# A hybrid transformer block: sums of squares from the feature-major x, the decay chain placed within the first projection

## The chip, the core and the metric

The kernel runs on one core of one Trainium2 chip, as one program. The time is device microseconds of one execution; the median of several is given. TensorE multiplies matrices, VectorE (DVE in the profile), ScalarE (ACT) and GpSimd (POOL) work element by element, and SyncE (SP) issues the loads.

## The reference

One block of a model works on 256 tokens of 2048 features, all in fp32. A token mixer joins a spatially gated MLP and a gated linear attention; cross attention to a memory and a convolutional feed-forward layer follow. What the change touches is at the start:

```python
h = rmsnorm(x, pre_norm_mix[l])            # x * rsqrt(mean(x*x) + 1e-6) * g
z = h @ w_in                               # all projections of the mixer
...
u, vs = jnp.split(gelu(z_sg), 2, axis=-1)
y_a = spatial_gating(u, layernorm(vs, sg_ln_g, sg_ln_b), sg_w, sg_b)
gate_logit = (g_lr @ gla_w_gate2 + gla_b_gate).astype(jnp.float32)   # rank 16
log_a = jnp.maximum(jax.nn.log_sigmoid(gate_logit) / GLA_TAU, GLA_LOG_DECAY_MIN)
...
bcum = jnp.cumsum(to_chunks(log_a), axis=3)    # chunks of 64 tokens
q_in = qc * jnp.exp(bcum); k_in = kc * jnp.exp(-bcum); k_st = kc * jnp.exp(b_last - bcum)
```

## The kernel before

The 256 tokens are two tiles of 128. The 2048 features are 16 groups (k) of 128 partitions, and x comes twice: as token rows (`x`) and feature-major (`xT`). Each fp32 product is made of three: weights and activations are split into a part `hi`, rounded by a cast on ScalarE (`split_half`, L89), and a rest `lo`, a subtraction on VectorE (L90). The products hi·hi, hi·lo and lo·hi are summed in PSUM (L106 to L108). The root mean square's factor is not applied to the activations: the products are made from x times the gain (`gain_x`, which fills `hT`), and the factor comes on afterwards, as a column per token tile (`rs`, tile `r_mix`) or, where tokens lie along the free axis, as a row copied to all partitions (`rbc`).

Weights come in units of 1 MB (three buffers). One unit is cut in two pieces of 1024 columns, so a piece is one cast, one subtraction and 12 matmuls of 512 columns. `hi` and `lo` have four buffers each: the cast of a piece reuses the buffer of the piece four before it.

The first stage is written out by hand (`tc.manual_schedule`): 8 rounds, each with one unit of `w_sgv`, for the half `v` of the gated MLP. In a round stand the load of a later unit, the splits, `square_x` and `load_x` of token rows of x, `later_loads` for constants, and 24 matmuls (L448). Behind the rounds come 16 matmuls for the gates' rank-16 input (`glr`, L452) and `row_bcast`, which makes `rbc` from the two columns by two fp32 matmuls with diagonals. Everything behind the stage is placed by a scheduler that orders each engine's instructions from the program and estimates of their times.

Next come the gelu of `v` with its layer norm (L467 to L483, on `vv`), and `tok_block(w_sg, 0)` and `(w_sg, 1)`, the half `u`, of eight pieces each. After each piece but the first, `tok_block` calls `step()`, which takes one function from the list `later`. There stand the four `gate` (two matmuls each, Abs on ScalarE and a minimum on VectorE), `decay` (Exp and Ln on 128x2048, subtraction, scale), `cums` (a scan along the tokens, then the differences that fill `E1`) and `powers(q)` (exponentials into `EK` and `E1`, one head a call). `powers` of heads 1 to 3 are called in the blocks of k and q, which follow.

Of the kernel before, what the change touches and what calls it, by code (L numbers as in the profile page):

```python
# [44 lines left out]
def block_kernel(ctx: ExitStack, tc: tile.TileContext, a, out):  # L45
# [269 lines left out]
    with ExitStack() as mix:  # L315
# [20 lines left out]
        with ExitStack() as st2:  # L336
            xp0 = pool(st2, "sp0", side="right")

            gmix = xp0.tile([P, KD], F32, name="gmix")
            xt = [xp0.tile([P, 2, S], F32, name=f"xt_{i}") for i in range(KD // 2)]  # L340
# [3 lines left out]
            gh1 = xp0.tile([48, S], F32R, name="gh1")  # L344
            g2 = uu[1][0:96, :]
            xh, ss4s, rs = {}, {}, []

            def load_xt(k, n, eng=nc.sync):
                eng.dma_start(out=xt[k // 2][:, k % 2:k % 2 + n, :], in_=a["xT"][:, k:k + n, :])

            def load_unit(parts=((slice(0, 2), slice(0, 2)),)):
                i = len(first)
# [1 line left out]
                for n, k in parts:  # L354
                    nc.sync.dma_start(out=first[i][:, n, k, :], in_=a["w_sgv"][i, :, n, k, :])

            def load_x(i):
                t, n = divmod(i, 4)
                xh[i] = xp0.tile([P, 512], F32, tag="xh", bufs=3, name=f"x0_{t}_{n}")
                nc.sync.dma_start(out=xh[i], in_=a["x"][t * P:(t + 1) * P, n * 512:(n + 1) * 512])  # L360

            def square_x(i):
                t, n = divmod(i, 4)
                if n == 0:
                    ss4s[t] = stat.tile([P, 4], F32, tag="ss4", name=f"ss4_mix_{t}")
                nc.scalar.activation(out=uu[0][:, 0:512], in_=xh[i], func=AF.Square, accum_out=ss4s[t][:, n:n + 1])
                if n == 3:
                    ss = stat.tile([P, 1], F32, tag="ss", name=f"ss_mix_{t}")
                    nc.vector.reduce_sum(out=ss, in_=ss4s[t], axis=AX.X)
                    rs.append(rstd_of(ss, 1.0 / D, f"mix_{t}", const.tile([P, 1], F32, name=f"r_mix_{t}")))  # L370

            def gain_x(k):
                split_psum(hT[:, k, 0, :], hT[:, k, 1, :], xt[k // 2][:, k % 2, :], scale=gmix[:, k:k + 1])

            def later_loads(i):
                if i == 3:
                    nc.sync.dma_start(out=ident, in_=a["eye"])
                    nc.sync.dma_start(out=cols, in_=a["cols"])
                if i == 5:
                    nc.sync.dma_start(out=sgw, in_=a["sg_wT"])  # L380
                    nc.gpsimd.affine_select(
                        out=sgw, in_=sgw, pattern=[[0, SGG], [1, P]], compare_op=ALU.is_ge,
                        fill=0.0, base=0, channel_multiplier=-1)
                if i == 4:
                    nc.sync.dma_start(out=wgr, in_=a["w_glr"])
                    nc.sync.dma_start(out=g2, in_=a["gate2"])
                if i == 6:
# [7 lines left out]
                    nc.sync.dma_start(out=lng, in_=a["sg_ln_g"].partition_broadcast(P))  # L395
                if i == 7:
                    nc.sync.dma_start(out=lnb, in_=a["sg_ln_b"].partition_broadcast(P))

            first = []
            with tc.manual_schedule():  # L400
                nc.scalar.dma_start(out=gmix, in_=a["cols"][:, C_MIX:C_MIX + KD])
                first.append(wpool.tile([P, 2, 2, 512], F32, tag="raw", bufs=3, name="raw"))
                for k in (0, 1):
                    for n in range(2):
                        nc.sync.dma_start(out=first[0][:, n, k, :], in_=a["w_sgv"][0, :, n, k, :])
                        if n == 0:
                            load_xt(k, 1)
                load_xt(2, 2, nc.scalar)
                load_unit([(slice(0, 2), k) for k in range(2)])
                load_xt(4, 2)  # L410
                load_unit()
                warm_up(10)
                pss = [[mm_psum(f"sg_{n}_{t}") for t in range(NT)] for n in (2, 3)]
                nx = 0
                for i in range(KD // 2):
                    if 1 <= i < KD // 2 - 2:
                        load_xt(2 * i + 4, 2)
                        load_unit()
                    hl = []
# [16 lines left out]
                    for j in sorted(xh):  # L436
                        if j >= nx:
                            square_x(j)
                    nx = len(xh)
                    for j in {2: (0, 1), 3: (2,), 4: (3, 4), 5: (5,), 6: (6, 7)}.get(i, ()):  # L440
                        load_x(j)
                    later_loads(i)
                    for k in (2 * i, 2 * i + 1):
                        c = slice(k % 2 * 512, (k % 2 + 1) * 512)
                        for n, (hi, lo) in enumerate(hl):
                            for j, (part, w) in enumerate(((0, hi), (1, hi), (0, lo))):
                                for t in range(NT):
                                    nc.tensor.matmul(pss[n][t], hT[:, k, part, t * P:(t + 1) * P], w[:, c],  # L448
                                                     start=k == 0 and j == 0, stop=k == KD - 1 and j == 2)
                ps = mm_psum("glr")  # L450
                for k in range(KD):
                    nc.tensor.matmul(ps[0:80, :], wg[:, k, :, :], hT[:, k, :, :], start=k == 0, stop=k == KD - 1)  # L452
                row_bcast(rs, rbc, "mix")
# [19 lines left out]

        for n, ps in enumerate(pss):
            sg_v(ps, n + 2)
        for t in range(NT):
# [8 lines left out]
        with ExitStack() as st2:  # L485
# [4 lines left out]
            nc.gpsimd.memset(keep, 1.0)  # L490
            nc.gpsimd.memset(keep[:, :, 0:1], 0.0)

            def gate(i):
                gps = aux_psum(f"gate_{i}")
                for j in range(2):
                    f = 2 * i + j
                    nc.tensor.matmul(gps[:, j * S:(j + 1) * S], gate2[:, f * P:(f + 1) * P], glr,
                                     start=True, stop=True)
                gv = gps.rearrange("p (f s) -> p f s", f=2)
                nc.scalar.activation(out=la[:, 2 * i:2 * i + 2, :], in_=gv, func=AF.Abs)  # L500
                nc.vector.tensor_scalar_min(mn[:, 2 * i:2 * i + 2, :], gv, 0.0)

            def decay():
                nc.scalar.activation(out=la, in_=la, func=AF.Exp, scale=-1.0)
                nc.scalar.activation(out=la, in_=la, func=AF.Ln, bias=1.0)
                nc.vector.tensor_tensor(out=la, in0=mn, in1=la, op=ALU.subtract)
                nc.vector.tensor_scalar(out=la, in0=la, scalar1=1.0 / 16.0, scalar2=-1.0, op0=ALU.mult, op1=ALU.max)

            def cums():
# [51 lines left out]
        with ExitStack() as st:  # L561
# [454 lines left out]
```

## Time and profile before

| what | value |
|---|---|
| time, median of 3 (lowest to highest) | 1661.28 us (1660.66 to 1661.56) |
| profiled execution: time, span | 1661.93 us, 1660.2 us |
| TensorE busy | 1646.9 us (99% of the span), 8086 matmuls |
| VectorE, ScalarE, GpSimd busy | 1042.1 us (63%), 846.1 us (51%), 39.8 us (2%) |
| HBM read | 314.08 MB, 190 GB/s over the span |

The profile's page gives busy times over the whole span. The ends of matmul records are modelled, so that the start of one matmul to the start of the next is the measure of TensorE's pace. A row of the timeline gives start, duration, engine, line, operation, out<-in, shape, a count where like rows are joined, and in brackets the engine's idle time before it and what ended it.

### The profile page before, as it was taken

What the parts mean: (1) busy time and instruction counts of PE and PEld (TensorE: products, weight loads), DVE (VectorE), ACT (ScalarE), POOL (GpSimd) and SP (SyncE); (2) the same over time, 40 slices, a digit from 0 to 9 for tenths busy, and PEclk for the clock granted to TensorE, in tenths of its full rate; (3) what the DMA queues carried; (4) which work ended last, traced back from release to release, by engine and by line L of the source; (5) the groups of instructions that cost most, each with busy time, mean ns of one, the idle gap of its engine ahead of it and who ended that gap; (6) DMA issues with size and microseconds to landing.
All of it is one profiled execution on the core that took longest, in us unless ns stands there. A gap on an engine that the chain in (4) does not pass through costs nothing.

```text
span 1660.2 us, 20835 instructions
## 1 busy us (share of the span) xinstructions
PE 1646.9 (99%) x8086; PEld 1374.8 (83%) x8086; DVE 1042.1 (63%) x1394; ACT 846.1 (51%) x1182; POOL 39.8 (2%) x128
## 2 busy tenths in 40 slices
PE   9999999999999999999999999999999999999998
PEld 7788888888888888888888888888888888888886
DVE  5777645555454545465766877877777787444444
ACT  6774444444444444455655756555555555344332
POOL 0100000000000000000002000000000000000000
PEclk9999999999999999999999999999999999999999
DMA  9545455445555554585542555555555555555553
GB/s 344 221 160 177 177 186 172 176 176 177 186 194 178 182 198 178 187 333 215 204 177 105 202 193 187 181 200 178 190 191 182 195 181 216 190 187 193 179 199 103
DMA packets 49139, 317.52 MB, mean 191 GB/s; under 512 B 5552, under 2 KB 6192, under 8 KB 12304
## 3 DMA queue, kind: packets, MB, share of 16 engines
q1 hardware_dynamic: 48752, 315.93, 53.4%
q8 instruction: 63, 1.03, 0.2%
q14 instruction: 36, 0.29, 0.1%
q10 hardware_dynamic: 288, 0.27, 0.0%
HBM read 314.08 MB, written 2.10 MB: 190 GB/s over the span
## 4 chain that ended last, share of the span: by engine, by line
PE 95%; DMA 2%; ACT 1%; issue 1%; DVE 1%; SPq 0%; DVEq 0%; POOLq 0%; POOL 0%; ACTq 0%
PE up L137 18%; PE up L138 10%; PE ffn L108 5%; PE ffn L107 5%; PE ffn L106 5%; PE m L108 4%; PE m L107 4%; PE m L106 4%; PE p L108 3%; PE p L106 3%; PE p L107 3%; PE mix L108 2%; PE mix L106 2%; PE og L107 2%; PE v L108 2%; PE og L106 2%
## 5 line engine op out<-in xcount | busy, mean ns | idle before, releaser
L90 DVE TENSOR_TENSOR lo<-raw,hi 128x1024 fp32r<-128x1024 f32 (+1 forms) x567 | 689.5, 1219 | 460.9 <-ACT hi L89 456.7
L89 ACT CAST hi<-raw 128x1024 fp32r<-128x1024 f32 (+1 forms) x568 | 590.5, 1043 | 534.4 <-PE ffn L107 133.6
L137 PE MATMUL up<-fT,hi 128*128 128x512 f32 x1320 | 467.3, 394 | 0.4 <-DVE fT L210 0.4
L138 PE MATMUL up<-fT,lo 128*128 128x256 f32 x1320 | 373.1, 283 | 0.0
L137 PEld LDWEIGHTS up<-fT,hi 128*128 128x128 f32 x1320 | 247.9, 188 | 54.3 <-DVE fT L210 0.7
L138 PEld LDWEIGHTS up<-fT,lo 128*128 128x128 f32 x1320 | 248.1, 188 | 3.9
L108 PE MATMUL ffn<-lo,act 128*128 128x512 f32 x352 | 140.1, 399 | 0.0
L107 PE MATMUL ffn<-hi,act 128*128 128x512 f32 x352 | 138.7, 394 | 0.0
L106 PE MATMUL ffn<-hi,act 128*128 128x512 f32 x352 | 138.0, 392 | 0.0
L893 ACT COPY hd<-up 128x256 f32<-128x256 f32 x88 | 32.7, 373 | 137.0 <-PE up L141 137.0
L106 PE MATMUL m<-hi,hT 128*128 128x512 f32 x256 | 101.4, 396 | 0.0
L108 PE MATMUL m<-lo,hT 128*128 128x512 f32 x256 | 101.3, 396 | 0.0
L107 PE MATMUL m<-hi,hT 128*128 128x512 f32 x256 | 101.1, 395 | 0.0
L894 DVE TENSOR_TENSOR hd<-up,hd 128x256 f32<-128x256 f32 x88 | 37.4, 425 | 72.4 <-ACT hd L893 72.4
L107 PEld LDWEIGHTS ffn<-hi,act 128*128 128x128 f32 x352 | 66.1, 188 | 17.2
L106 PEld LDWEIGHTS ffn<-hi,act 128*128 128x128 f32 x352 | 66.1, 188 | 15.7
L108 PEld LDWEIGHTS ffn<-lo,act 128*128 128x128 f32 x352 | 66.1, 188 | 15.3
L107 PEld LDWEIGHTS m<-hi,hT 128*128 128x128 f32 x256 | 48.1, 188 | 11.4
L108 PEld LDWEIGHTS m<-lo,hT 128*128 128x128 f32 x256 | 48.1, 188 | 11.4
L106 PEld LDWEIGHTS m<-hi,hT 128*128 128x128 f32 x256 | 48.1, 188 | 11.2
L897 ACT ACTIVATE cv<-hd,cols 128x256 f32<-128x256 f32 x88 | 52.7, 602 | 0.3
L106 PE MATMUL v<-hi,hT 128*128 128x512 f32 x128 | 51.1, 399 | 0.0
(301 smaller groups left out, 2480.1 us busy)
## 6 DMA issues: line engine op xcount, KB each, us to landing
raw<-in_w_up SPq DMA_DIRECT2D x88, 1024.0 KB, 4.8
raw<-in_w_dn SPq DMA_DIRECT2D x44, 1024.0 KB, 4.8
raw<-in_w_v SPq DMA_DIRECT2D x16, 1024.0 KB, 4.8
raw<-in_w_og SPq DMA_DIRECT2D x16, 1024.0 KB, 4.8
raw<-in_w_ma SPq DMA_DIRECT2D x16, 1024.0 KB, 4.8
raw<-in_w_mb SPq DMA_DIRECT2D x16, 1024.0 KB, 4.8
raw<-in_w_pb SPq DMA_DIRECT2D x16, 1024.0 KB, 4.8
raw<-in_w_o SPq DMA_DIRECT2D x16, 1024.0 KB, 4.9
```

Of the source, the lines that this page charges most:

```text
L89: nc.scalar.copy(out=hi, in_=raw)
L90: (eng or nc.vector).tensor_tensor(out=lo, in0=raw, in1=hi.bitcast(F32), op=ALU.subtract)
L106: nc.tensor.matmul(ps, xh, wh, start=first, stop=False)
L107: nc.tensor.matmul(ps, xl, wh, start=False, stop=False)
L108: nc.tensor.matmul(ps, xh, wl, start=False, stop=last)
L137: nc.tensor.matmul(*big, start=k == 0, stop=False)
L138: nc.tensor.matmul(*small, start=False, stop=False)
L893: nc.scalar.copy(out=hd[:, 2:], in_=ps[:, S:2 * S])
L894: nc.vector.tensor_tensor(out=hd[:, 2:], in0=ps[:, 0:S], in1=hd[:, 2:], op=ALU.add)
L897: nc.scalar.activation(out=cv, in_=hd[:, 2:], func=AF.Identity, scale=cols[:, w0 + 2:w0 + 3], bias=cols[:, C_CB + j:C_CB + j + 1])
```

## The change

It has three parts. The squares are summed from the feature-major `xT`, which is loaded anyway: one ScalarE Square for each pair of k (128x512), added up on VectorE into `acc`. Before the last k of the first projection `token_rstd` adds the two halves and multiplies by ones on TensorE, in fp32: twice 128x2 for the columns, once 128x256 for the row on all partitions. VectorE scales both, and GpSimd raises them to the power -0.5, 128x2 into `rr` and 128x256 into `rbc`. The loads of `x` in this stage, their Squares with accumulate and `row_bcast` go.

Second, loads of constants move behind other weight units, `xt` becomes one tile that is loaded in fewer pieces, and the selection on `sgw` stands behind the stage.

Third, the gates, `decay`, `cums` and all four `powers` are put in `later` ahead of block 0, the four gates as one function `gates`, and TensorE's order in block 0 is that of the program. The gates' sums stay in PSUM until `decay`, which takes the minimum in one operation with the subtraction. The layer norm comes into the program behind block 0.

```diff
+            acc = xp0.tile([P, 2, S], F32, name="acc")
+            msb = xp0.tile([P, S], F32, name="msb")
...
-            def load_x(i):
-                t, n = divmod(i, 4)
-                xh[i] = xp0.tile([P, 512], F32, tag="xh", bufs=3, name=f"x0_{t}_{n}")
-                nc.sync.dma_start(out=xh[i], in_=a["x"][t * P:(t + 1) * P, n * 512:(n + 1) * 512])
-
             def square_x(i):
...
+                sq = acc if i == 0 else xp0.tile([P, 2, S], F32, tag="sq", bufs=2, name="sq")
+                nc.scalar.activation(out=sq, in_=xt[:, 2 * i:2 * i + 2, :], func=AF.Square)
+                if i > 0:
+                    nc.vector.tensor_tensor(out=acc, in0=acc, in1=sq, op=ALU.add)
+
+            def token_rstd():
+                nc.vector.tensor_tensor(out=acc[:, 0, :], in0=acc[:, 0, :], in1=acc[:, 1, :], op=ALU.add)
+                tot = aux_psum("tot")
+                for t in range(NT):
+                    nc.tensor.matmul(tot[:, S + 2 * t:S + 2 * t + 2], acc[:, 0, t * P:(t + 1) * P], ones[:, 0:2],
+                                     start=True, stop=True)
+                nc.tensor.matmul(tot[:, 0:S], ones, acc[:, 0, :], start=True, stop=True)
+                ms = stat.tile([P, NT], F32, tag="ms2", name="ms_mix")
+                nc.vector.tensor_scalar(out=ms, in0=tot[:, S:S + 2 * NT:2], scalar1=1.0 / D, scalar2=EPS,
+                                        op0=ALU.mult, op1=ALU.add)
+                nc.vector.tensor_scalar(out=msb, in0=tot[:, 0:S], scalar1=1.0 / D, scalar2=EPS,
+                                        op0=ALU.mult, op1=ALU.add)
+                nc.gpsimd.tensor_tensor(out=rr, in0=ms, in1=neg_half, op=ALU.pow)
+                nc.gpsimd.tensor_tensor(out=rbc, in0=msb, in1=neg_half[:, 0:1].to_broadcast([P, S]), op=ALU.pow)
...
                     for k in (2 * i, 2 * i + 1):
+                        if k == KD - 1:
+                            token_rstd()
...
-                row_bcast(rs, rbc, "mix")
...
             def gate(i):
-                gps = aux_psum(f"gate_{i}")
+                gps = mm_psum(f"gate_{i}")
...
-                nc.vector.tensor_scalar_min(mn[:, 2 * i:2 * i + 2, :], gv, 0.0)
+                gvs.append(gv)
...
-                nc.vector.tensor_tensor(out=la, in0=mn, in1=la, op=ALU.subtract)
+                for i, gv in enumerate(gvs):
+                    part = la[:, 2 * i:2 * i + 2, :]
+                    nc.vector.scalar_tensor_tensor(out=part, in0=gv, scalar=0.0, in1=part, op0=ALU.min, op1=ALU.subtract)
...
-            later += [partial(gate, i) for i in range(4)] + [decay]
-            sg_u(tok_block(a["w_sg"], 0, hT, KD, "sg"), 0)
+            def gates():
+                for i in range(4):
+                    gate(i)
+
+            later += [lambda: None, gates, decay, cums] + [partial(powers, q) for q in range(H)]
+            with tc.manual_schedule(engines={mybir.EngineType.PE}):
+                ps = tok_block(a["w_sg"], 0, hT, KD, "sg")
             flush()
-            later += [cums, partial(powers, 0)]
+            sg_u(ps, 0)
+            later += [partial(layer_norm, t) for t in range(NT)]
...
-                if h < H - 1:
-                    later.insert(0, partial(powers, h + 1))
```

Where the scheduler puts the gates is seen in the order of each engine. The first two pieces show TensorE in block 0 of the first projection's half `u`, first before, then after. `sg_0_0` and `sg_0_1` are the block's sums for the two token tiles, `hi_666` and `hi_579` pieces of the weights, `glr_84` the gates' input; the numbers differ between the kernels.

```order
L106 MATMUL sg_0_0_579<-hi_666,hT_76 128x512
L107 MATMUL sg_0_0_579<-hi_666,hT_76 128x512
L108 MATMUL sg_0_0_579<-lo_667,hT_76 128x512
L497 MATMUL gate_0_615<-glr_84,gate2_85 128x256 x2
L497 MATMUL gate_1_638<-glr_84,gate2_85 128x256 x2
L106 MATMUL sg_0_1_580<-hi_666,hT_76 128x512
```

```order
L107 MATMUL sg_0_1_542<-hi_579,hT_76 128x512
L108 MATMUL sg_0_1_542<-lo_580,hT_76 128x512
L503 MATMUL gate_0_595<-glr_84,gate2_85 128x256 x2
L503 MATMUL gate_1_599<-glr_84,gate2_85 128x256 x2
L503 MATMUL gate_2_603<-glr_84,gate2_85 128x256 x2
L503 MATMUL gate_3_607<-glr_84,gate2_85 128x256 x2
L106 MATMUL sg_0_0_541<-hi_611,hT_76 128x512
```

Before, four gate matmuls stand inside the fifth piece and four more in the next but one; after, all eight stand between the third piece (`hi_579`) and the fourth (`hi_611`).

ScalarE at the same place, after the change; the casts L463 to L465 make `glr`, and `hi_680` takes the buffer that `hi_579` had (four pieces earlier).

```order
L89 CAST hi_636<-raw_634 128x1024
L89 CAST hi_660<-raw_634 128x1024
L89 CAST hi_680<-raw_678 128x1024
L463 CAST glr_84<-gl1_106 32x256
L464 CAST glr_84<-gl1_106 16x256
L465 CAST gh1_107<-gl1_106 16x256
L506 ACTIVATE la_534<-gate_0_595 128x512
```

Before, the three casts stand directly behind the cast of the fifth piece, `hi_666`, whose matmuls are those ahead of the gates; now they stand behind that of the seventh piece, with the gates' Abs next.

VectorE, after the change, from the subtraction of the seventh piece to the third one behind the gates; L461 multiplies by `rbc`, L466 is the last write of `glr`, L484 and L486 are the layer norm, L518 is the scan.

```order
L90 TENSOR_TENSOR lo_681<-raw_678,hi_680 128x1024
L461 TENSOR_TENSOR gl1_106<-gl1_106,rbc_83 80x256
L484 TENSOR_SCALAR vv_0_91<-vv_0_91,mv_0_757,rs_ln_0_761 128x1024
L484 TENSOR_SCALAR vv_1_92<-vv_1_92,mv_1_784,rs_ln_1_788 128x1024
L486 TENSOR_TENSOR vv_0_91<-vv_0_91,lng_96 128x1024
L466 TENSOR_TENSOR glr_84<-gl1_106,gh1_107 16x256
...
L514 SCALAR_TENSOR_TENSOR la_534<-gate_3_607,la_534 128x512
L90 TENSOR_TENSOR lo_699<-raw_678,hi_698 128x1024
L515 TENSOR_SCALAR la_534<-la_534 128x2048
L90 TENSOR_TENSOR lo_726<-raw_723,hi_725 128x1024
L518 SCALAR_TENSOR_TENSOR mn_535<-keep_536,la_534 128x2048
L90 TENSOR_TENSOR lo_742<-raw_723,hi_741 128x1024
```

Before, the multiplication by `rbc` (L457 there) stands ahead of `lo_667`, the subtraction of the fifth piece, and the scan stands in block 1, some 25 us behind the gates.

## Rows read from the trace of the kernel before

**Rows 1.** The page, busy time, share of the span and instructions of each engine.

```profile
PE 1646.9 (99%) x8086; PEld 1374.8 (83%) x8086; DVE 1042.1 (63%) x1394; ACT 846.1 (51%) x1182; POOL 39.8 (2%) x128
```

**Rows 2.** Timeline of TensorE, four places.

```profile
45.29 0.63 PE L448 MATMUL sg<-lo,hT 128*128 128x512 f32 x2
46.24 1.19 PE L448 MATMUL sg<-hi,hT 128*128 128x512 f32 x4 [0.32 <-ACT hi L89]
47.79 0.73 PE L448 MATMUL sg<-lo,hT 128*128 128x512 f32 x2 [0.36 <-DVE lo L90]
...
56.26 0.38 PE L181 MATMUL rb_mix<-dg_mix,ones 128*128 128x128 f32 x2
...
112.30 1.05 PE L537 MATMUL sps<-vv,sgw 128*128 128x128 f32 x8
113.78 0.49 PE L137 MATMUL q<-hT,hi 128*128 128x512 f32 x1 [0.42 <-ACT hi L89]
115.03 0.39 PE L138 MATMUL q<-hT,lo 128*128 128x256 f32 x1 [0.76 <-DVE lo L90]
...
138.11 1.28 PE L568 MATMUL att<-QT,KT 128*128 128x128 f32 x10
```

**Rows 3.** Timeline of ScalarE, 41 to 107 us.

```profile
41.55 0.63 ACT L366 ACTIVATE uu<-x 128x512 f32<-128x512 f32 x1 [2.59 <-DMA x<-in_x]
...
63.52 1.05 ACT L89 CAST hi<-raw 128x1024 fp32r<-128x1024 f32 x1
...
70.39 1.09 ACT L500 ACTIVATE la<-gate 128x512 f32<-128x512 f32 x2 [1.46 <-PE gate L497]
...
78.73 1.28 ACT L504 ACT_TABLE_LOAD   x1
80.03 1.92 ACT L504 ACTIVATE la<-la 128x2048 f32<-128x2048 f32 x1
...
103.86 2.20 ACT L530 ACTIVATE EK<-E 128x512 f32<-128x512 f32 x4
...
106.89 3.90 ACT L531 ACTIVATE E<-E 128x1024 f32<-128x1024 f32 x4
```

**Rows 4.** Timeline of VectorE, five places.

```profile
54.57 1.27 DVE L468 BATCH_NORM_STATS2 bst<-vv 128x6 f32<-128x512 f32 x2
...
59.96 0.80 DVE L480 TENSOR_SCALAR vv<-vv,mv,rs_ln 128x1024 f32<-128x1024 f32 x1
...
61.81 0.41 DVE L457 TENSOR_TENSOR gl<-gl,rbc 80x256 f32<-80x256 f32 x1
...
63.28 1.21 DVE L90 TENSOR_TENSOR lo<-raw,hi 128x1024 fp32r<-128x1024 f32 x1
...
95.48 4.42 DVE L510 TENSOR_TENSOR_SCAN mn<-keep,la 128x2048 f32<-128x2048 f32 x1
...
806.00 5.39 DVE L275 SCALAR_TENSOR_TENSOR x<-x,rsy_mix,xr 128x512 f32<-128x512 f32 x8 [0.32 <-POOL rsy_mix L270]
...
888.20 1.92 DVE L90 TENSOR_TENSOR lo<-raw,hi 128x1024 fp32r<-128x1024 f32 x1 [1.44 <-ACT hi L89]
```

**Rows 5.** Timeline of GpSimd, from the start to 893 us.

```profile
0.80 0.10 POOL L63 MEMSET neg_half<- 128x2 f32 x1 [0.29 <-POOLq L1006]
...
51.48 0.56 POOL L154 TENSOR_TENSOR r_mix<-ms_mix,neg_half 128x1 f32<-128x1 f32 x1 [7.88 <-DVE ms_mix L152]
56.21 2.39 POOL L154 TENSOR_TENSOR rs_ln<-ms_ln,neg_half 128x1 f32<-128x1 f32 x2 [4.17 <-DVE ms_ln L152]
...
886.35 6.03 POOL L90 TENSOR_TENSOR fT<-raw,fT 128x1024 fp32r<-128x1024 f32 x2 [68.37 <-ACT fT L89]
892.72 2.41 POOL L90 TENSOR_TENSOR lo<-raw,hi 128x1024 fp32r<-128x1024 f32 x1 [0.34 <-ACT hi L89]
```

**Rows 6.** A stretch at the end: length, each engine's busy time, granted clock, DMA.

```profile
1656.00:1661.00 5.00, 0.00 (x0) 0.00 (x0) 0.34 (x1) 0.00 (x0) 0.00 (x0) 0.50 0.47 150
```

**Rows 7.** Loads of the first 150 us: count, KB each, median us to landing.

```profile
x<-in_x SPq DMA_DIRECT2D x8, 256.0 KB, 10.0
```

More of the change, by code (lines that the diff above doesn't have):

```diff
@@ L339, in block_kernel @@
             gmix = xp0.tile([P, KD], F32, name="gmix")
-            xt = [xp0.tile([P, 2, S], F32, name=f"xt_{i}") for i in range(KD // 2)]
+            xt = xp0.tile([P, KD, S], F32, name="xt")
+            acc = xp0.tile([P, 2, S], F32, name="acc")
             wgr = xp0.tile([P, KD, 16], F32, name="glr_raw")
@@ L344, in block_kernel @@
             gh1 = xp0.tile([48, S], F32R, name="gh1")
+            msb = xp0.tile([P, S], F32, name="msb")
+            rr = const.tile([P, NT], F32, name="r_mix")
+            rs = [rr[:, t:t + 1] for t in range(NT)]
             g2 = uu[1][0:96, :]
-            xh, ss4s, rs = {}, {}, []
             def load_xt(k, n, eng=nc.sync):
-                eng.dma_start(out=xt[k // 2][:, k % 2:k % 2 + n, :], in_=a["xT"][:, k:k + n, :])
+                eng.dma_start(out=xt[:, k:k + n, :], in_=a["xT"][:, k:k + n, :])
             def load_unit(parts=((slice(0, 2), slice(0, 2)),)):
@@ L355, in load_unit @@
                     nc.sync.dma_start(out=first[i][:, n, k, :], in_=a["w_sgv"][i, :, n, k, :])
-            def load_x(i):
-                t, n = divmod(i, 4)
-                xh[i] = xp0.tile([P, 512], F32, tag="xh", bufs=3, name=f"x0_{t}_{n}")
-                nc.sync.dma_start(out=xh[i], in_=a["x"][t * P:(t + 1) * P, n * 512:(n + 1) * 512])
             def square_x(i):
[L363 to L370, printed above, removed]
+                sq = acc if i == 0 else xp0.tile([P, 2, S], F32, tag="sq", bufs=2, name="sq")
@@ L372, in gain_x @@
             def gain_x(k):
-                split_psum(hT[:, k, 0, :], hT[:, k, 1, :], xt[k // 2][:, k % 2, :], scale=gmix[:, k:k + 1])
+                split_psum(hT[:, k, 0, :], hT[:, k, 1, :], xt[:, k, :], scale=gmix[:, k:k + 1])
             def later_loads(i):
-                if i == 3:
+                if i == 2:
+                    nc.sync.dma_start(out=wgr, in_=a["w_glr"])
+                    nc.sync.dma_start(out=g2, in_=a["gate2"])
+                if i == 5:
+                    nc.sync.dma_start(out=sgw, in_=a["sg_wT"])
+                    nc.sync.dma_start(out=lng, in_=a["sg_ln_g"].partition_broadcast(P))
@@ L377, in later_loads @@
+                if i == 6:
+                    nc.sync.dma_start(out=lnb, in_=a["sg_ln_b"].partition_broadcast(P))
                     nc.sync.dma_start(out=ident, in_=a["eye"])
                     nc.sync.dma_start(out=cols, in_=a["cols"])
[L379 to L383, printed above, removed]
@@ L384, in later_loads @@
                 if i == 4:
-                    nc.sync.dma_start(out=wgr, in_=a["w_glr"])
-                    nc.sync.dma_start(out=g2, in_=a["gate2"])
-                if i == 6:
                     for j in range(5):
@@ L394, in later_loads @@
                                             op=ALU.subtract)
-                    nc.sync.dma_start(out=lng, in_=a["sg_ln_g"].partition_broadcast(P))
-                if i == 7:
-                    nc.sync.dma_start(out=lnb, in_=a["sg_ln_b"].partition_broadcast(P))
             first = []
@@ L402, in block_kernel @@
                 first.append(wpool.tile([P, 2, 2, 512], F32, tag="raw", bufs=3, name="raw"))
[L403 to L408, printed above, removed]
+                for n in range(2):
+                    nc.sync.dma_start(out=first[0][:, n, 0, :], in_=a["w_sgv"][0, :, n, 0, :])
+                    load_xt(n, 1)
+                nc.sync.dma_start(out=first[0][:, :, 1, :], in_=a["w_sgv"][0, :, :, 1, :])
+                load_xt(2, 2)
                 load_unit([(slice(0, 2), k) for k in range(2)])
-                load_xt(4, 2)
+                load_xt(4, 4)
                 load_unit()
+                load_xt(8, 4)
                 warm_up(10)
                 pss = [[mm_psum(f"sg_{n}_{t}") for t in range(NT)] for n in (2, 3)]
-                nx = 0
                 for i in range(KD // 2):
                     if 1 <= i < KD // 2 - 2:
-                        load_xt(2 * i + 4, 2)
                         load_unit()
+                    if i == 1:
+                        load_xt(12, 4)
                     hl = []
@@ L435, in block_kernel @@
                             split_half(first[i][:, n, :, :].rearrange("p k c -> p (k c)"), into=x)
[L436 to L441, printed above, removed]
+                    square_x(i)
                     later_loads(i)
                     for k in (2 * i, 2 * i + 1):
+                        if k == KD - 1:
+                            token_rstd()
                         c = slice(k % 2 * 512, (k % 2 + 1) * 512)
@@ L452, in block_kernel @@
                     nc.tensor.matmul(ps[0:80, :], wg[:, k, :, :], hT[:, k, :, :], start=k == 0, stop=k == KD - 1)
-                row_bcast(rs, rbc, "mix")
+            nc.gpsimd.affine_select(
+                out=sgw, in_=sgw, pattern=[[0, SGG], [1, P]], compare_op=ALU.is_ge,
+                fill=0.0, base=0, channel_multiplier=-1)
             nc.scalar.copy(out=gl1, in_=ps[0:80, S:2 * S])
@@ L475, in block_kernel, with layer_norm @@
             sg_v(ps, n + 2)
-        for t in range(NT):
+        def layer_norm(t):
             mv = stat.tile([P, 2], F32, tag="mv", name=f"mv_{t}")
@@ L491, in block_kernel @@
             nc.gpsimd.memset(keep[:, :, 0:1], 0.0)
+            gvs = []
             def gate(i):
-                gps = aux_psum(f"gate_{i}")
+                gps = mm_psum(f"gate_{i}")
                 for j in range(2):
```

## The prediction

> **What bounds the kernel now.** I read the page first: TensorE is busy 99% of the span [rows 1], so time moves only where TensorE stands still or gets matmuls more or fewer. The change touches only the first 140 us. There I read TensorE's timeline by starts, because the ends of its records are modelled. Back to back, a 512-column matmul starts 0.2325 us after the last: four take 0.93 us and the twelve of one piece (1024 columns of the weights, both token tiles) 2.79 us. Anything above that pitch is a stall. [Rows 2] hold the places: from 45.29 two matmuls should take 0.47 us, yet the next starts 0.95 us later; from 46.24 four should take 0.93 us, the next starts 1.55 us later. That is 0.48 + 0.62, about 1.1 us, and with 0.1 after it 1.2 us. Later, eight small matmuls from 112.30 are issued by 113.2, the next starts at 113.78, and the one after that at 115.03 in place of 114.01: 0.6 + 1.0, and with 0.2 in the rows behind 1.8 us. A stall of 0.5 us near 101 is of the same kind. Each names a cast on ScalarE or the subtraction on VectorE that cuts a weight piece in hi and lo.
>
> Next I read who makes those late. At 41.55 ScalarE has sat 2.59 us for a token load, whose Square stands ahead of the casts in its order, and four conversions follow [rows 3]. The token loads land a median 10.0 us after their issue [rows 7]: they queue behind 1 MB weight units on the same queue. The 113 us stall comes from ScalarE's burst of 2.20 + 3.90 + 1.28 us of exponentials and a table load, from 103.86 to 112.1 [rows 3].
>
> **The change, part by part.** *Sums of squares.* Eight loads, eight Squares with accumulate and the two reductions go. What comes is 8 Squares of 128x512 and 7 additions in the eight rounds, spread, and nothing waits for a load that the projection doesn't need anyway. I count the 1.2 us at 45 to 48 as gone. Price on TensorE: three fp32 products inside the last k. Ten records of fp32, 128 columns, take 1.28 us [rows 2], some 0.11 us a record net, two records to a product. The 128x256 product is about 0.44 us, the two of 2 columns together 0.2 to 0.5: 0.65 to 0.95, with the changes between forms up to 1.3; I take 1.0. The sum `acc` is complete at about 43 us and TensorE there at 48, so it doesn't wait. The broadcast's two products leave (0.44 us, and 0.17 for their changes of form): -0.6. The first product starts at most 0.25 us earlier, as `xt` of k=1 stands one transfer ahead; I take -0.1.
>
> *Gates as one bunch.* This is the largest term. All eight gate matmuls now stand behind the third piece of block 0 (of `hi_579`), and TensorE's order is fixed. What they wait for: ScalarE's order has the cast `hi_680` ahead of the casts that make `glr`; `hi_680` takes the buffer of `hi_579`, so it can't begin before TensorE has finished that very piece. VectorE has `lo_681` ahead of the multiplication by `rbc`, and two normalizations and a product by `lng` ahead of the last write of `glr`. So from the end of the third piece, in order: cast 1.05, subtraction 1.21, product 0.34 (0.41 less its overlap), two normalizations 2 x 0.72 (0.80 less overlap), product by `lng` 1.14 (as long as a subtraction), last write of `glr` 0.41 [rows 3, 4]. That is 5.6 us during which TensorE has nothing that it may run. In the order of before, two more pieces (5.6 us) stand there.
>
> *The chain behind the gates,* from their start G: first pair 0.25, four Abs 2.1, Exp and Ln with a table load each 2 x (1.28 + 1.92), G+8.75 [rows 3]; four min-and-subtract of 128x512 by 0.67 (the row of eight at 806) [rows 4], less overlap 2.5, G+11.25; subtraction, scale and subtraction 3 x 1.15, scan 4.42, subtraction `lo_742` 1.15 [rows 4]: G+20.2. TensorE wants `lo_742` after 0.94 (gates) + 6 pieces (16.74) + 4 matmuls (0.93) + one small one (0.22) = G+18.8: a stall of 1.4. Then ScalarE: three copies, table load, gelu, cast, table load, four EK (2.20), cast, four E1 (3.90), cast `hi_827` at about G+32.9; TensorE, with the 1.4 in it, comes at G+31.1: 1.7, split over two casts. Together +3.1. What this buys: no exponentials are left for the k and q stage, so the 1.8 at 113 and the 0.5 at 101 go, -2.3.
>
> *Clock.* At the end of the kernel, with TensorE idle, the granted clock is 0.50 [rows 6], which is 1.2 GHz where 2.4 was granted all along. No row shows it inside the program. If it falls during the 5.6 us, some matmuls behind it run at half pace: nothing if it doesn't, a piece's 2.8 us if it lasts one piece. Half of that, and most is taken back, because the later stalls wait for ScalarE and VectorE and not for TensorE: +0.5.
>
> *Power of 128x256 on GpSimd,* which makes `rbc` in place of diagonal, matmul and copy. No row has it. Of one column it takes 0.56 us, where a fill that small takes 0.10 [rows 5]. A lower bound is the per-element pace of a GpSimd subtraction, 2.41 us for 1024: 0.56 + 255 x 2.35 ns = 1.15 us. An upper bound is 256 times the 0.46 us above the fill: 118 us. The ends lie a factor of 100 apart; a power is many steps an element, but the 0.46 us hold start-up too, so I take the geometric middle, about 11, as 10 us. It starts at about 50.2 us: the three products end at 49.4, two scalings and the power of two columns come first. `rbc` itself is wanted only at 66 us, so 10 us would seem hidden. But a GpSimd tensor operation and a VectorE one of two inputs exclude each other: at 888.20 a VectorE subtraction took 1.92 us in place of 1.21 beside GpSimd's pair that ran 6.03 us in place of 2 x 2.41 [rows 4, 5]. With that, `lo_580` and all behind it wait; ahead of `lo_681`, for which ScalarE is ready at 65.1, stand four subtractions, four statistics of 0.63, 0.9 us of small operations and the norm's two powers of 2.39 together [rows 4, 5], which hold VectorE in the same way: 4.6 + 2.5 + 0.9 + 2.4 = 10.4 us. The free allowance is so 65.1 - 50.2 - 10.4 = 4.5 us, and each further us moves the gates by one: 10 us cost +5.5.
> The Trainium skill ("SBUF — State Buffer", § Who interferes with whom) says that VectorE and GpSimd share a port pair, as an exclusive lock held for a whole instruction: the trace agrees (the 1.92). Without it the allowance would be some 16 us, and the time 1667.3. The skill's "GPSIMD Engine Reference" (§ 3.1) puts a two-input operation at some 2.6 cycles an element, by which, as my estimate, 256 elements take 0.55 us more than one, which would give 1667.3 too; the cycle count there is for an addition, and no run here shows it for a power.
>
> *Constants' loads* move among weight units; the same bytes less 2.1 MB, at most of use against waits that I've counted; 0. `lng` lands before 60 us, ahead of its use at 68; were it 2 us later than that, the gates would move with it.
>
> Sum without the power: +5.6 + 3.1 + 1.0 + 0.5 - 1.2 - 0.6 - 2.3 - 0.1 = +6.0. With it +11.5. The profiled execution took 1661.93 us (span 1660.2 and 1.7 around it), 0.65 above the median of 1661.28, so I add to the median: 1667.3 with a hidden power, **1672.8** with 10 us.
>
> **Rivals.** *(a) The power is hidden (5 us or less):* 1667.3, own range 1664.5 to 1669. For it: GpSimd's 2.35 ns an element in a subtraction; against it: that a power isn't one step, and 0.46 us for one column.
> *(b) The power is long (over 20 us):* 25 us give 15 more than the forecast, 1687.8; 40 us give 1702.8; the upper bound 118 us about 1781. For it: 0.46 us of one column, if that were mostly work; against it: that start-up must be in it.
> *(c) Not slower.* The mechanism is that the chain behind the gates ends sooner than TensorE needs it, so that the +3.1 doesn't come, with a hidden power: 6.0 - 3.1 = +2.9, within 0.2% of before. It decides if ScalarE and VectorE run from the gates to `lo_742` in under 18.8 us in place of 20.2, and to `hi_827` in under 31.1. To be faster by over 0.2% the bunch must also find `glr` ready: the wait of 5.6 would have to fall under some 0.3 us, which only another order than the one shown could do. For (c): all durations carry some 0.1 us each over 20 links; against it: both chains are sums of rows of this kernel.
> *(d) The loads don't matter:* if the 1.2 us at 45 stay, because the Squares of `xt` and the conversions still stand ahead of the casts, every case is 1.2 higher, inside each range.
>
> **How the numbers follow.** What a measurement here can tell from no change is about 0.2%, 3.3 us: same is 1658 to 1664.6. Chances: forecast (power of 5 to 20 us, 1667.5 to 1683) 0.42; (a) 0.28; (b) 0.18; (c) 0.12, of which 0.04 is faster. Of (a), 0.02 falls below 1664.6 as well. Faster 0.04, same 0.10, slower 0.86. The likeliest one's own range is 1667.5 to 1683. For 8 in 10 I leave out about 0.1 below (most of (c)) and 0.1 above (half of (b)): 1664 to 1698.
>
> **What would show it.** Right: TensorE's wait for the first gate matmul is 5.6 us or more and names VectorE's write of `glr`; the row of GpSimd's 128x256 power has about 10 us, with a subtraction on VectorE (`lo_580`) stretched beside it; two stalls in block 1 on `lo_742` and on casts near the exponentials; none from k on; none at 45 to 48; the fp32 products cost about 1 us. Wrong: the power under 5 us gives (a), over 20 (b). Most exposed is the one operation without a row; next, whether the order holds VectorE to `lo_681` ahead of `rbc`'s product on the chip.

## The result, and the profile after

The changed kernel took 1678.83 us (median of 4 runs, 1677.99 to 1680.09), the kernel before 1661.30 (1660.66 to 1661.56): 1.0107 times as long, 95% interval 1.0089 to 1.0124. The prediction was 1672.8 with a range of 1664 to 1698, and slower. It is slower, by 1.1%. The profiled execution took 1679.23 us, with a span of 1677.5.

The page gives the same matmuls (two more) in less busy time than before [rows 1]: 1631.3 us in place of 1646.9, though the span is 17.3 us longer.

```profile
PE 1631.3 (97%) x8088; PEld 1373.5 (82%) x8088; DVE 1044.1 (62%) x1397; ACT 845.5 (50%) x1173; POOL 79.5 (5%) x128
```

The waits of TensorE in the first 150 us (engine, line, what it waited for: us in total, times, longest) say where the loss is: one wait of 31.4 us for the last write of `glr`, and small ones at the start and behind the gates.

```profile
PE gate L503 <- DVE glr L466: 31.4, 1, 31.4
PE sg L450 <- ACT hT L189: 1.9, 3, 0.9
...
PE sg L108 <- DVE lo L90: 1.1, 2, 0.6
PE sg L106 <- ACT hi L89: 1.0, 2, 0.7
```

GpSimd's timeline has the operation that no row of before had. Two columns take 0.70 us, where one took 0.56 [rows 5], and 256 take 41.14: 40.44 us for 254 more, 0.159 us each.

```profile
50.78 0.70 POOL L378 TENSOR_TENSOR r_mix<-ms_mix,neg_half 128x2 f32<-128x2 f32 x1 [12.73 <-DVE ms_mix L374]
51.45 41.14 POOL L379 TENSOR_TENSOR rbc<-msb,neg_half 128x256 f32<-128x256 f32 x1
```

VectorE's timeline beside it and behind it. The subtractions of two inputs that ran beside the power took 1.22 to 1.23 us, as without it (1.21) [rows 4]. From 67.18 to 92.62 VectorE waits for `rbc`, and from there its order goes as written: the product at 92.62, two normalizations, a product by `lng`, the write of `glr` at 96.01.

```profile
52.47 1.23 DVE L90 TENSOR_TENSOR lo<-raw,hi 128x1024 fp32r<-128x1024 f32 x1 [1.51 <-ACT hi L89]
...
65.96 1.22 DVE L90 TENSOR_TENSOR lo<-raw,hi 128x1024 fp32r<-128x1024 f32 x1 [1.49 <-ACT hi L89]
92.62 0.42 DVE L461 TENSOR_TENSOR gl<-gl,rbc 80x256 f32<-80x256 f32 x1 [25.44 <-POOL rbc L379]
93.14 1.70 DVE L484 TENSOR_SCALAR vv<-vv,mv,rs_ln 128x1024 f32<-128x1024 f32 x2
94.76 1.22 DVE L486 TENSOR_TENSOR vv<-vv,lng 128x1024 f32<-128x1024 f32 x1
96.01 0.42 DVE L466 TENSOR_TENSOR glr<-gl,gh 16x256 fp32r<-16x256 f32 x1
```

TensorE at the same place: its last matmul of the third piece starts at 64.69, the first gate at 96.48. The matmuls behind it start 0.43 us apart in place of 0.23, until about 100. The windows (start and end, length, busy time of each engine, granted clock) show why: the granted clock is 0.50, that is 1.2 GHz in place of 2.4, from 70 to 100, behind a stretch in which TensorE stood still, and 1.00 from 100.

```profile
64.69 0.39 PE L108 MATMUL sg<-lo,hT 128*128 128x512 f32 x1
96.48 2.08 PE L503 MATMUL gate<-glr,gate 96*128 96x256 f32 x8 [31.41 <-DVE glr L466]
98.35 0.63 PE L106 MATMUL sg<-hi,hT 128*128 128x512 f32 x1
98.78 0.63 PE L107 MATMUL sg<-hi,hT 128*128 128x512 f32 x1
```

```profile
70.00:80.00 10.00, 0.00 (x0) 0.00 (x0) 0.00 (x0) 0.00 (x0) 10.00 (x1) 0.50 0.00 0
90.00:100.00 10.00, 3.52 (x12) 3.20 (x13) 7.10 (x8) 3.83 (x8) 5.96 (x5) 0.50 0.00 0
100.00:110.00 10.00, 10.00 (x45) 8.26 (x44) 4.08 (x6) 8.68 (x7) 0.00 (x0) 1.00 0.00 0
```

At the first matmul of the `v` projection the changed kernel is 33.3 us late (237.34 against 204.02 us). At the last matmul of the program it is only 17.3 us late (1668.84 against 1651.54), in stages that the diff doesn't touch. The rows of one line's matmuls (count, shortest, median and longest in ns, first and last start) show it in `v`, first before, then after: 128 matmuls of one line lie between 204.0 and 370.0, 166.0 us, and between 237.3 and 399.5, 162.2 us, with the same matmuls of other blocks among them. From start to start a 512-column matmul of `v` takes 0.2328 us before and 0.2274 after; the granted clock is 1.00 in both.

```profile
L106 PE MATMUL v<-hi,hT x128: 390/393/477, 204.0 to 370.0; 128*128 128x512 f32 x128
```

```profile
L106 PE MATMUL v<-hi,hT x128: 387/389/481, 237.3 to 399.5; 128*128 128x512 f32 x128
```

So there are two things to settle: what makes up the 33.3 us, and why TensorE is faster everywhere else.

### The profile page after: what moved, and what is told of

Same layout as the page of the kernel before. It is cut to its first block, busy times and chain, and to the rows that moved or that the text cites. A ratio compares the mean times of both kernels' runs of the same rounds, so it can differ in the third digit from the quotient of the medians.

```text
span 1677.5 us, 20806 instructions
## 1 busy us (share of the span) xinstructions
PE 1631.3 (97%) x8088; PEld 1373.5 (82%) x8088; DVE 1044.1 (62%) x1397; ACT 845.5 (50%) x1173; POOL 79.5 (5%) x128
## 4 chain that ended last, share of the span: by engine, by line
PE 91%; ACT 1%; issue 1%; DVE 1%; POOL 0%; DVEq 0%; POOLq 0%; ACTq 0%
PE up L137 18%; PE up L138 9%; PE ffn L106 5%; PE ffn L108 5%; PE ffn L107 5%; PE m L106 3%; PE m L108 3%; PE m L107 3%; PE p L106 3%; PE p L108 3%; PE p L107 3%; PE mix L108 2%; PE mix L107 2%; PE v L106 2%; PE v L108 2%; PE v L107 2%
```

## The experiments

**The power and the order.** The first theory is that the power is too long, doesn't hold VectorE, and that the order alone costs 5.6 us. In this run GpSimd raises 96 of the 256 columns.

```diff
-                nc.gpsimd.tensor_tensor(out=rbc, in0=msb, in1=neg_half[:, 0:1].to_broadcast([P, S]), op=ALU.pow)
+                nc.gpsimd.tensor_tensor(out=rbc[:, 0:96], in0=msb[:, 0:96], in1=neg_half[:, 0:1].to_broadcast([P, 96]), op=ALU.pow)
+                nc.scalar.copy(out=rbc[:, 96:S], in_=msb[:, 96:S])
```

> The changed kernel with GpSimd's power on 96 of the 256 columns; the other 160 are copied on ScalarE, so that their values are not the root. The order around the gates is that of after. By the rate of the trace (0.70 us for 2 columns, 41.14 for 256: 0.159 us each) the power takes 15.6 us and ends at about 67, when the last subtraction ahead of its reader does. Theory C (the power does not hold VectorE up, and the order alone costs 5.6 us): TensorE's wait at the gates falls from 31.6 to 5.6 us, and the time to about 1678.8 - 26 - 1.5 (less time at half clock) = 1651, between 1649 and 1654. The prediction's theory (VectorE's subtractions of two inputs wait for the power): the wait is 5.6 + 15.6 - 4.5 = 16.7 us and the time about 1662. Rival (the wait is the power's alone, the order costs nothing): wait under 1 us, 1646.

It took 1657.54 us (0.9974 of before, 0.9965 to 0.9984). The power's row is 15.64 us and ends at 66.63; VectorE's product by `rbc` starts at 66.67, directly behind its subtraction. The wait at the gates is 5.9 us.

```profile
50.99 15.64 POOL L379 TENSOR_TENSOR rbc<-msb,neg_half 128x96 f32<-128x96 f32 x1
```

```profile
PE gate L504 <- DVE glr L467: 5.9, 1, 5.9
PE sg L106 <- ACT hi L89: 3.4, 2, 1.8
PE sg L451 <- ACT hT L189: 1.8, 2, 1.0
```

That is the 5.6 us of the order, without any hold of VectorE (which would have given 16.7) and with the power's end hidden. The time is 6 us above the expected 1651 (5 in the profiled execution), mostly since two things came dearer than expected: half clock behind a wait of only 5.9 us, with the gates and nine matmuls of 0.43 us in it (2.8 us in all, where 1.5 less than in the changed kernel was expected), and 5.4 us of later stalls (by starts) in place of 3.5 in the changed kernel. The order further on is not quite that of the changed kernel: ScalarE has the second gelu between the two groups of exponentials here, at the price of two more table loads, and the cast `hi` behind them is later by as much.

```profile
98.33 1.28 ACT L477 ACT_TABLE_LOAD   x1
99.63 0.69 ACT L477 ACTIVATE uu<-sg,r_mix 128x512 f32<-128x512 f32 x1
...
101.27 1.28 ACT L540 ACT_TABLE_LOAD   x1
```

Next, the power of 128x256 and its product leave altogether; `row_bcast` stands behind the `glr` matmuls again, and the rest of the change stays.

```diff
-                nc.tensor.matmul(tot[:, 0:S], ones, acc[:, 0, :], start=True, stop=True)
-                nc.gpsimd.tensor_tensor(out=rbc, in0=msb, in1=neg_half[:, 0:1].to_broadcast([P, S]), op=ALU.pow)
...
+                row_bcast(rs, rbc, "mix")
```

> The changed kernel without GpSimd's power of 128x256 and its product: rbc is made by row_bcast, behind the glr matmuls as before the change; gates, decay and loads stay as changed. With no power to wait for, the order has the multiplication by rbc and the casts of glr ahead of the splits of pieces 5 to 7, so that glr is ready before the third piece ends. Theory C: no wait at the gates, 5.9 us and some 2.8 us at half clock less than with the power on 96 columns, of which the later stalls take back about as much as the half clock gave: 1657.5 - 5.9 = about 1651.5, between 1648 and 1654. Rival (the bunch of gates is what costs): a wait of 5 us remains and the time is 1656 to 1658.

It took 1642.97 us, 0.9890 of before (0.9874 to 0.9907), faster than either kernel and than expected. All waits of TensorE in its first 150 us, without that of the warm-up:

```profile
PE sg L445 <- ACT hT L189: 0.7, 2, 0.4
PE sg L108 <- DVE lo L90: 0.3, 1, 0.3
```

There is no wait at the gates, and of the chain behind them one of 0.3 us is left. In this kernel's order the product by `rbc` stands three subtractions earlier, and `glr` is written at 60.04, 3.8 us ahead of the first gate matmul.

```profile
57.45 0.42 DVE L457 TENSOR_TENSOR gl<-gl,rbc 80x256 f32<-80x256 f32 x1
60.04 0.41 DVE L462 TENSOR_TENSOR glr<-gl,gh 16x256 fp32r<-16x256 f32 x1
```

So the late place of that product in the changed kernel came with the power: there the scheduler put what depends on `rbc` behind other work. Bunch and power aren't independent costs.

**TensorE's pace.** The diff makes one constant tile out of two (32 bytes a partition less) and adds a tag of four 32-byte buffers. In the built programs the weight buffers thereby stand 32 bytes lower and `hT` 96 higher. The first theory was that the place modulo 64 matters.

```diff
+    pad = const.tile([P, 8], F32, name="pad")
+    nc.gpsimd.memset(pad, 0.0)
```

> The kernel before with one unused constant tile of 32 bytes a partition (and its fill), so that the weight buffers raw, hi, lo and the activations hT stand 32 bytes higher, at 32 modulo 64 in place of 0, as they do after the change; the order on every engine is that of before. Theory A (the pace of TensorE's 512-column matmuls depends on where the operands lie): a pitch of 0.227 us in place of 0.233 in the projections, and about 1661.3 - 16.0 (gained in the trace after the change from the v projection on) - 2 (some 380 matmuls of the first stages by 6 ns) = 1643, between 1640 and 1647. Theory B (the pace differs for another reason, such as the changed order or the long wait): 0.233 us and 1661.3, within 1.5.

It took 1660.16 us (0.9991 of before, 0.9982 to 1.0000), with `v` as slow as before. The theory fell: the places modulo 64 were those of the changed kernel, and the pace wasn't. With the pad behind the weight buffers:

> The kernel before with a 32-byte tile behind the weight buffers: raw, hi and lo stay at 0 modulo 64, hT and what lies on it move to 32. If theory A holds and the moving operand decides (hi and lo in the token-major projections), the pitch stays at 0.233 us and the time within 4 us of 1661.3; in the feature-major up projection, where hT's successor fT moves, it changes. If the loaded weights decide (hT there), the pitch is 0.227 and the time about 1643 to 1647. Theory B: 1661.3.

It took 1656.13 us (0.9966, 0.9952 to 0.9980). `v` didn't gain, the up projection did: 491.8 us from first to last start in place of 496.7. And the changed kernel with the first pad:

> The changed kernel with the same 32-byte constant tile: raw, hi, lo and hT go back to 0 modulo 64, as before the change. Theory A: 1678.8 + 18 = 1697, between 1693 and 1700, with a pitch of 0.233 us. Theory B: 1678.8, within 1.5.

It took 1684.72 us (1.0137 of before, 1.0122 to 1.0152), 12 less than expected. Its `v` kept the fast pace; mix and ffn, the output projections of the mixer and of the feed-forward layer, went back to the pace of before. What fits all of them is the distance between the two operands that TensorE reads, the moving one and the loaded weights, modulo 256. The places of the built programs, in bytes of a partition, and the starts of the trace:

```
kernel                 hi      hT      (hi - hT) mod 256   v: us from first to last start
before                 44096   79040   128                 166.40
pad in the constants   44128   79072   128                 166.42
pad behind the weights 44096   79072    96                 166.65
changed, with pad      44096   79168     0                 162.55
changed                44064   79136     0                 162.59
```

That theory forecast the next two kernels: the kernel before, with a pad of 128 bytes behind the weight buffers, and with one of 128 bytes ahead of both.

```diff
+    pad = stat.tile([P, 32], F32, tag="pad", bufs=1, name="pad")
+    nc.gpsimd.memset(pad, 0.0)
```

> The kernel before with hT and what lies on it 128 bytes higher (79168 in place of 79040), the weight buffers where they were. Theory A2 (the pace goes with the distance of the moving operand from the loaded weights, modulo 256: 0 gave 0.227 us in the changed kernel, 128 gave 0.2325 before, in the projections where hi and lo move and hT is loaded): the distance is 0 now, so 0.227 us from the first projection to p; by the stages of the changed kernel with the pad, 12.8 us less from v to the mix projection, 2 to 3 less ahead of it, and 3.3 more in the up projection, where fT moves: 1649 to 1651. Theory A3 (the place of hT alone decides, 64 modulo 128 and modulo 256 as before): for a period of 128 no change, 1661; for a longer one the same 1650. Theory B (addresses don't matter): 1661.7.

It took 1651.07 us (0.9939, 0.9925 to 0.9954), at the upper end of the 1649 to 1651 of the distance. Its `v`:

```profile
L108 PE MATMUL v<-hi,hT x128: 389/389/477, 205.0 to 367.1; 128*128 128x512 f32 x128
```

The gain lies from `v` on: 9.9 us up to the last matmul, by starts, where 9.5 was expected. Ahead of `v`, where 2 to 3 was expected, the profiled execution (1653.03 us, the longest of four) gained nothing: `v` starts 1.0 us later than before, as TensorE's waits there, without that of the warm-up, add up to 4.9 us in place of 2.5.

In this kernel the weight buffers and the activations stand where they stand in the changed kernel with the pad. From the first matmul of `v` to the last of the program the one takes 1437.6 us and the other 1437.7, so that the places account for all of the difference in pace. At equal places the change as it stands costs 33.7 us (1684.72 - 1651.07), and not 17.5.

> The kernel before with weight buffers and hT both 128 bytes higher, so that hT stands at 79168 as in the run before this one, and its distance from hi at 128 modulo 256 as in the kernel before. Theory A2 (distance): 0.2325 us in the first 700 us, no gain there. Theory A3 (place of hT): 0.227 us there and some 12 to 15 us less. In mix and ffn the distance is a new one (224 modulo 256), whose pace neither theory knows.

It took 1662.12 us (1.0003, 0.9994 to 1.0012); `hT` stands at 79168 as in the run ahead of it, but the distance is 128 again, and with it the old pace:

```profile
L108 PE MATMUL v<-hi,hT x128: 390/393/477, 204.0 to 369.8; 128*128 128x512 f32 x128
```

The place of `hT` alone is ruled out. Then the pace by itself, on TensorE alone:

> None of the block is computed: x is copied to the output, and TensorE runs 24 matmuls for each place of the moving operand and of the loaded weights, in steps of 32 bytes, with all else idle; then pairs of 512 and 256 columns as in the feature-major projections. Theory A2: the pitch depends on the difference alone and repeats with 256 bytes: moving the weights by some bytes gives what moving the operand by as many in the other direction gives, and moving both changes nothing. Theory A3: it follows one of the places. If it is flat at one pitch, the pace comes from what the other engines do on the same memory, and not from TensorE's own two reads.

From the starts of the trace, mean ns from one 512-column matmul to the next, by the distance (moving less weights) in bytes; in the first line the moving operand was shifted, in the second the weights. The last line is a pair of 512 and 256 columns with other weights.

```
distance mod 256        0      32     64     96     128    160    192    224
moving shifted        226.7  233.4  229.3  233.9  233.5  234.0  233.5  233.1
weights shifted       227.7  233.4  229.3  233.4  233.5  233.9  233.4  233.1
pair of 512 and 256   351.8  347.4  351.3  350.8  350.8  347.5  352.5  352.7
```

Distances of 256 to 480 repeated the first line within 1 ns, and 512 to 8192 gave 226.7 to 226.8. Moving both by 128 bytes changed nothing beyond 1 ns (226.9 at a distance of 0). So the pace comes from the places of TensorE's own two operands, with the other engines idle: a distance of 0 is 2.9% faster than most others, 64 is 1.8% faster; for the feature-major pair 32 and 160 are best.

**Put to use, and the rest of the change by itself.** The kernel with `row_bcast`, with unused tiles that set the distances of later stages:

```diff
+        mpool.tile([P, 48], F32, name="pad_mpool")
...
+    ftp.tile([P, 8], F32, name="pad_ftp")
...
+        fp.tile([P, 48], F32, name="pad_fp")
```

> The changed kernel with row_bcast (the run of 1643 us) and three unused tiles that move the later activations, with the same order on every engine: mT and act 192 bytes lower, so that their distance to the weight buffers is 0 modulo 256 in place of 64, fT 32 bytes higher, so that it is 32 in place of 0. Theory A2 by the rows of the kernel that only varied the distance (0.2267 us at 0, 0.2293 at 64; pairs of the feature-major form 347.4 ns at 32 and 352.7 at 0): up 1320 pairs by 5.3 ns or more, 7 to 8.2 us less; ffn 1056 by 2.6 ns, 2.7 us; mix 384 by 2.6, 1.0 us: 1643.0 - 11 to 12 = 1631 to 1632. Rival (the pace in these stages is set by more than the distance): within 3 us of 1643.

It took 1632.33 us (0.9823, 0.9808 to 0.9837), against 1631 to 1632 forecast: up 492.6 us in place of 499.9, ffn 239.2 in place of 241.5. One line of ffn, in the changed kernel and here:

```profile
L106 PE MATMUL ffn<-hi,act x352: 392/394/397, 1427.3 to 1668.4; 128*128 128x512 f32 x176
```

```profile
L106 PE MATMUL ffn<-hi,act x352: 389/389/402, 1382.2 to 1620.9; 128*128 128x512 f32 x176
```

> The kernel before, its order unchanged, with four unused tiles that set the distances: 0 modulo 256 where hT, mT and act are loaded, 32 where fT moves. Theory A2: from the run with hT moved (1651.1) up 8.2 less, mix 2.8 and ffn 7.4 less: 1632.7, between 1631 and 1635. The rest of the change, with row_bcast, is then worth the difference to the same kernel with favourable places, 1 to 2 us.

It took 1635.91 us (0.9842, 0.9827 to 0.9856), 3 above the forecast. So at equal distances the source change without the power is worth some 3.6 us (1635.91 - 1632.33); the intervals of the two ratios overlap. The two profiled executions (1637.16 and 1631.78 us) have the difference ahead of `v`, which starts at 205.55 here and at 199.93 there; from `v` to the last matmul they take 1421.1 and 1421.4 us. Some of it is the clock: in the kernel before with these places TensorE waits 1.7 us for a cast and 0.4 for a subtraction between 45 and 48 us, and behind that the granted clock is 0.50 for 3.4 us, which costs 1.6.

```profile
48.50:51.90 3.40, 3.40 (x9) 2.64 (x8) 3.37 (x6) 2.25 (x5) 0.03 (x1) 0.50 0.50 160
```

> Of the change only the sums of squares from xT and the loads, with row_bcast for rbc; gates, decay, cums, powers and the layer norm stand as in the kernel before. Places as after the change, so the pace is the same as in the run of 1643 us, and the difference to it is the placement of the decay chain alone. From rows: the chain of before costs stalls of 0.5 near 100 and 1.8 near 113, in place of 0.7 near 93: 1643.0 + 1.6 = 1644.6, between 1643 and 1646. Rival (placing the chain early is worth nothing or costs): 1643 or less.

It took 1644.92 us (0.9897, 0.9882 to 0.9911). Against 1642.97 the intervals overlap, so the times don't settle it; in the profiled executions the `v` projection starts at 203.16 us here and at 200.40 with the decay chain early. By the medians the chain's placement is worth 2 us and by these two executions 2.8, if `rbc` is early.

The last run has the favourable places and puts the first loads back:

```diff
-                for n in range(2):
-                    nc.sync.dma_start(out=first[0][:, n, 0, :], in_=a["w_sgv"][0, :, n, 0, :])
-                    load_xt(n, 1)
-                nc.sync.dma_start(out=first[0][:, :, 1, :], in_=a["w_sgv"][0, :, :, 1, :])
-                load_xt(2, 2)
+                for k in (0, 1):
+                    for n in range(2):
+                        nc.sync.dma_start(out=first[0][:, n, k, :], in_=a["w_sgv"][0, :, n, k, :])
+                        if n == 0:
+                            load_xt(k, 1)
+                load_xt(2, 2, nc.scalar)
```

> The run with row_bcast and favourable places, and the first loads as before the change (the second pair of xT on ScalarE's queue, unit 0 in four loads): the stalls of TensorE between 8 and 15 us, 1.1 us in the run of 1643 and 1.8 to 2.1 us in the changed kernel, go: about 1 us less than that run, 1630 to 1631. Rival (those stalls come from ScalarE's Squares of xT, which stay): no difference.

It took 1631.29 us (0.9817, 0.9800 to 0.9833), 1.0 less than without it, as forecast, though the two intervals overlap. In the profile the stalls between 8 and 15 us are gone. This is the fastest kernel of the study, 31 us below before.

## Why the prediction held, and where its reasons did not

The sign and the range held, and the likeliest time was 6 us short. But that was luck: two terms were far off, with opposite signs, and a third was missing, so the time is no evidence for the sum. By the prediction's own signs rival (b) came true, a power of over 20 us, and its price for 40 us was 1702.8. From 1672.8 the way to the measured time is +31.1 for the length of the power, -10.6 for the hold of VectorE that didn't come (a wait of 31.6 in place of 42.2), -18.4 for TensorE's pace and +3.6 for the smaller terms below, together 1678.5.

- **The bunch of gates, +5.6:** right as a term of the order. With the power out of the way it measured 5.9. In the changed kernel 3.9 of it (92.59 to 96.48) stand behind the power's end and the rest lies beside it, so 31.6 us is one wait, not two.
- **The power of 128x256, 10 us:** this size failed. It measured 41.14 us. The geometric middle of 1.15 and 118 us was a choice without a row, too small by a factor of 4; the upper bound, which took the 0.46 us of one column for work alone, was too large by a factor of 2.9. No row of the kernel before could tell them apart. Two columns in one operation could have: they cost 0.14 us more than one.
- **VectorE held by the power:** this step failed too. The prediction took the row at 888.20, beside a GpSimd subtraction, for a rule on all GpSimd operations. Beside the power VectorE's subtractions took 1.22 to 1.23 us. The Trainium skill ("SBUF — State Buffer", § Who interferes with whom) has the pair of ports locked for a whole instruction; for this instruction the trace differs, and the measurement decides. By the prediction's own sum 41.1 us would have given about 1703.9. Without the hold, the power was hidden until about 66 us, and it ended at 92.6: that is the other 26 us. Rows of the kernel before already pointed that way. The norm's two powers, which the prediction counted as 2.39 us of hold [rows 5], took 1.51 and 0.91 us, where one by itself takes 0.56; the subtraction that ran beside the first took 1.23 us, as ever. So it was the power that got longer there, and not VectorE.

```profile
56.09 1.23 DVE L90 TENSOR_TENSOR lo<-raw,hi 128x1024 fp32r<-128x1024 f32 x1
```

```profile
L154 POOL TENSOR_TENSOR rs_ln<-ms_ln,neg_half x2: 912/1209/1506, 56.2 to 57.7; 128x1 f32<-128x1 f32 x2
```

- **The chain behind the gates, +3.1:** 3.5 us of stalls by starts (0.9 at `lo_742`, 2.6 at two later pieces). Nothing is left at 101 and 113 us, as forecast.
- **The clock, +0.5:** 1.8 us at half pace in the changed kernel and 2.8 with the power on 96 columns, so the term was 1.3 to 2.3 us too small.
- **The products for the sums, +1.0:** from 49.39 to 50.08 and 0.2 behind it, 0.9. **The stall at 45 to 48, -1.2,** is gone. **The start, -0.1:** the first matmul is 0.1 earlier, but two later ones wait for `hT`, +2.1 in all; merged and re-queued first loads, by the last run.
- **No term at all for TensorE's pace:** -16.0 us from `v` to the end and some 2.4 in the first stages (some 384 matmuls by 6 ns). The prediction said that all the change does lies in the first 140 us. It also moved operands.

For the time up to `v`: 31.6 + 1.8 + 3.5 + 2.1 + 0.9 - 0.1 - 4.2 (the removed stalls and `row_bcast`, by starts) - 2.4 = 33.2, against 33.3 measured.

The rival of a hidden power (1667.3) had the wrong price as well: the run with 96 columns, whose power is hidden, took 1657.5 with the new pace, so some 1676 with the old one. The half clock, the later stalls (5.4, with two further table loads ahead of them) and the start make most of the difference.

What stays open is why a power on GpSimd leaves VectorE alone where a subtraction did not; no run varied that.

## What to carry to other kernels

An operation without a row is the first thing to measure, and its price isn't only its own time: the order with the power and the one without it differed in the place of everything that waits for its result. Where TensorE is busy 99% of the time, compare its pace from start to start in stages that the diff doesn't touch; a changed tile size moves every operand behind it, and up to 6 ns a matmul came to 18 us here, five times what the change gains without its power. Such a difference must be taken out (same places in both) before two versions are compared.

## What the runs showed of the hardware that was not expected

- A power of fp32 on GpSimd: 0.159 us a column of 128 partitions (0.70 us for 2, 15.64 for 96, 41.14 for 256), 68 times the 2.35 ns of a subtraction [rows 5].
- TensorE's pace at a granted clock of 1.00 depends on the distance of its two operands modulo 256 bytes: 226.7 ns to 234.0 for 512 columns, 347.4 to 352.7 for a pair of 512 and 256, with the other engines idle.
- Half clock behind a wait of 5.9 us: the granted clock was 0.50 (1.2 GHz) in the stretch from 70 to 76 us of the run with 96 columns. In the kernel before with favourable places it was 0.50 from 48.5 to 51.9 us, behind waits of 1.7 and 0.4 us.

```profile
70.00:76.00 6.00, 5.48 (x17) 4.71 (x18) 3.93 (x5) 4.57 (x6) 1.96 (x2) 0.50 0.00 0
```
